# The first layer's expert outputs of three quads by way of DRAM rows instead of one-hot products

## The chip, the cores and the metric

One core of a Trainium2 chip runs the whole program. The metric is the device time of one execution in microseconds. The kernel before takes 940.01 us, the median of three runs (939.11 to 942.62).

## What is computed

Two trunk layers over 256 latent tokens (x) and 256 context tokens, 1024 channels, float32. Each layer ends in a mixture of experts; in the first layer all 512 tokens go through it. A token goes to one of four groups and to two of the group's four experts:

```python
eid = g * EXPERTS_PER_GROUP + ie                       # two experts of a token
gates = jnp.sum(jax.nn.one_hot(eid, N_EXPERTS) * wts[..., None], axis=1)
y = jnp.zeros_like(h)
for e in range(N_EXPERTS):
    a = jax.nn.silu(h @ w_gate[e]) * (h @ w_up[e])
    y = y + gates[:, e:e + 1] * (a @ w_down[e])
...
x = x + g2 * out[:B * N].reshape(B, N, D)
xc = xc + cg2 * out[B * N:].reshape(B, L, D)
```

An expert has 512 inner channels, so each of its three matrices is 2 MB and a layer's experts are 96 MB.

## The kernel before, in words

The change lies in `experts(l, ...)` with l = 0, the first layer. The 16 experts are taken in four **quads** q = 0 to 3 of four. A pair (token, expert) has a *slot*: an expert has 96, of which the first 64 of the four experts make slot tiles 0 and 1 of 128 rows, and the last 32 of each make tile 2. Tile 2 runs only where an expert of the quad has more than 64 pairs (`beyond(q)`, a branch; with these inputs in quads 1 and 2). Pairs beyond 96 are done after quad 1 by `overflow` (line 951), behind a branch on the count.

Per quad there are four chunks of 2 MB of gate weights (wg), four of up (wu) and four of down (wd). `weights` and `load` (line 108) fetch a chunk by a DMA on SP into a ring of five buffers and a sixth; a DMA into a buffer waits until PE has released what was in it six chunks ago. So SP runs at most six chunks ahead of PE.

`tiles` (line 1137) issues the products: gate into `ga`, then up into `ua`, then, after silu, product and transposes (line 172), down into `da`, one bank of 512 columns for each slot tile and half `hf` of the 1024 output channels. For a quad's inputs, `slots` (line 1066) builds a one-hot matrix `SS` of slot by token, `fetch` (lines 1079 to 1090) gathers the slots' rows of `h2d` in DRAM with indirect DMAs on POOL, and `turn` transposes them to channel-major `XT`.

The outputs go back to tokens with products. `halves` (lines 1253, 1254) splits a bank of `da` into a high part `oh` (ACT) and a low part `ol` (DVE), so that the product is exact. `combine` (line 1271) multiplies both parts by `SS`, 512 tokens at a time, which sums a token's two slots. `add` adds that into the channel-major x, times g2, with DVE (line 1291) or with ACT and POOL (lines 1288, 1289).

The order: a quad's first half is combined while its second half's down products run or right after them (line 1271 in the `if hf:` branch). Quad 1's second half is combined at once; those of quads 0 and 2 are left in `pending` and are emitted amid the next quad's gate products. Quad 3 goes by columns, and its combining is last. A scheduler places each instruction in an engine's queue; an engine runs its queue in order.

All weight DMAs are SP's; ACT issues a few of its own (rows of h2 to DRAM before the experts). Hardware-queue DMAs of SP and ACT share eight semaphores in turn, and a DMA waits for the one that had its semaphore before.

Of the kernel before, what the change touches and what calls it, by code (L numbers as in the profile page):

```python
# [36 lines left out]
EXTRA = 1  # slots for weights that the last layer's experts have besides the ring's and the early ones  # L37
CAP = {0: 96, 1: 64}

# columns of the packed small parameters  # L40
PAR_BMOD, PAR_NG, PAR_WR, PAR_BR, PAR_PSC = 0, 96, 128, 448, 488
PAR_W = 492
# columns of the constants that stay
CO_ID, CO_ONE, CO_TOK, CO_SLOT, CO_BEFORE, CO_BASE, CO_QUAD, CO_FIRST = 0, 128, 256, 768, 788, 804, 836, 840
CO_W = 844
# columns of the constants of the mixers
MC_ROT, MC_MASK = 0, 512
MC_W = 768
# columns of what pooling and the transform take, of both kinds
MB_POOL, MB_DFT, MB_CB, MB_PW, MB_FW = 0, 1088, 1600, 1856, 2112  # L50
BAND = 136  # tokens that a tile of 128 tokens reaches through the widest window
# columns of the per-layer parameters of the mixers
# [4 lines left out]
def build(tc, ctx, a, cap=CAP):  # L57
# [7 lines left out]
    shd = dram.tile([1, 2 * D], F32, name="shd")  # the first layer's second shift  # L65
    h2d = dram.tile([T, D], F32, name="h2d")  # rows of h2
    gd = dram.tile([T, 4], F32, name="gd")  # the slots and the gates
# [13 lines left out]
    class pinned:  # L81
        """an engine whose instructions stay in program order"""
# [37 lines left out]
    def load_split_parts(src, pinned=False, pool=None):  # L120
        """a generator of the two parts, after each chunk"""
# [25 lines left out]
    # the two streams, channel-major; the context's lives until the last layer has its keys and values  # L147
# [10 lines left out]
    count = cst.tile([P, 256], BF16, name="count")  # upper | ones, exact  # L158
# [15 lines left out]
    def keep_warm(n, bank=tmp):  # L174
        """products that nothing reads: TensorE's clock stays up over a wait"""
# [5 lines left out]
    def mod_stretch(l, st, pool, pinned=(), given=()):  # L181
        """a generator: yields after each piece of TensorE's work; given: pools for the first chunks, which are taken by
        themselves"""
# [25 lines left out]
        in_rows = l == 0 and st == 1  # the shift of the second norm goes to rows in DRAM  # L209
# [35 lines left out]
    class Squares:  # L245
        """sums of squares over the channels, taken as the chunks of x become final"""
# [27 lines left out]
        def rstd(self):  # L274
            """1 / rms of the tokens on their partitions"""
# [6 lines left out]
    def spread(out, x, pool, tag, bufs):  # L282
        """x [P, m] -> out [P, m * P]: the values along the free axis, on every partition"""
# [7 lines left out]
    # the first norm: h = x * rstd * s1 + sh in two parts  # L291
# [32 lines left out]
    def mixers(l, keep, pool, rb, w01, mods, box):  # L324
        """yields the chunks of x that are final"""
# [14 lines left out]
        def hs(k, t0, t1):  # L340
            """the two parts of tokens t0 .. t1"""
# [8 lines left out]
        # q | k | v, token-major  # L350
# [36 lines left out]
        # q and k: norm, rotary, to channel-major  # L387
        # q^T k of their parts: (hi lo) with (hi hi) and with (lo lo)
# [8 lines left out]
        def heads(tt):  # L397
# [13 lines left out]
            # the heads with their gains and, of the latents, turned  # L411
# [19 lines left out]
            # the parts: of k hi hi of each head, lo lo of each, of q lo hi | hi lo  # L431
# [29 lines left out]
        # pool | fourier, token-major  # L461
# [5 lines left out]
        # the rotary factors take the gains of q and k  # L467
# [8 lines left out]
        # after which products a tile's heads are turned  # L476
# [10 lines left out]
        # of the two tiles of a stream the transform takes the sum, for the even frequencies, and the difference, for the odd  # L487
# [9 lines left out]
        # attention: heads c and 4 + c, of the two kv heads, at a time  # L497
# [39 lines left out]
        def turned(tt, c, pr):  # L537
            """the probabilities with the keys on the partitions"""
# [14 lines left out]
        def attend():  # L553
# [3 lines left out]
            def start(i):  # L557
                """scores up to the i-th pair"""
# [84 lines left out]
        # output projection and gated residual: first the rows of pool and fourier, then attention's  # L643
# [25 lines left out]
    class Router:  # L669
        """logits = rstd * (x^T (s1 * w)) + sh^T w + b, taken as the chunks of x become final"""  # L670
# [682 lines left out]
    for l in range(L):  # L1353
# [8 lines left out]
        with phase(f"mix{l}", "right") as pool:  # L1362
# [49 lines left out]
            if l == 0:  # L1412
                drain(ro.plans)
# [164 lines left out]
```

## Time and profile before

| | |
|---|---|
| runs, median (range) | 940.01 us (939.11 to 942.62) |
| the profiled execution, its span from first to last instruction | 940.8 us |
| mean granted TensorE clock | 0.975 |
| busy: PE, DVE, ACT, POOL | 870.2, 410.6, 265.8, 64.3 us |
| DMA | 287.14 MB, mean 305 GB/s |
| quads 0, 1, 2, 3 of the first layer | 268.0 to 332.3, to 422.1, to 506.5, to 564.6 us |

The profile is one execution, whose span is the time that the sums below start from. PE is the matrix engine, PEld its weight load, DVE, ACT and POOL the vector, scalar and general engines, SP the one that issues the weight DMAs. A clock of 1.00 is TensorE's full speed. "idle before <-X" is idle time of an engine just ahead of an instruction and what ended it.

### The profile page before, as it was taken

To read this page: it belongs to the slowest core of one execution; us is meant where nothing else is said; L and a number is where in the kernel's file an instruction comes from. 1 tells how busy PE (TensorE), PEld (TensorE's weight loads), DVE (VectorE), ACT (ScalarE), POOL (GpSimd) and SP (SyncE) were. 2 spreads that over 40 slices of the span, in tenths; PEclk is the share of its full clock that TensorE was granted. 3 is DMA by queue.
4 is the path that set the end of the run, shared out by engine and by line. 5 is a ranking of instruction groups with operands and counts; after the bars stand their busy time and mean duration, and the time that the engine had idled before them with its cause. 6 is when DMAs were issued, how large, how long until landed. Compare 5 with 4: busy or idle time off the path is not lost. (4 is left out here: it accounts for less than half of the span.)

```text
span 940.8 us, 13190 instructions
## 1 busy us (share of the span) xinstructions
PE 870.2 (92%) x5078; PEld 480.7 (51%) x5078; DVE 410.6 (44%) x1028; ACT 265.8 (28%) x579; POOL 64.3 (7%) x74
## 2 busy tenths in 40 slices
PE   2899999999589999989999998989999999979998
PEld 2388666676253333442344446846874444424436
DVE  2285677723965240431122138877655231312212
ACT  4143667514421100110011035566432010101101
POOL 1000000001410030012001020000000000000000
PEclk9999999999599999999999997999999999989999
DMA  9636572653969999757966972894978999999981
GB/s 356 270 128 251 212 286 109 257 225 111 380 238 427 428 371 425 309 222 297 416 248 261 397 283 110 342 420 160 344 308 324 428 418 430 426 391 426 428 301 46
DMA packets 33393, 287.14 MB, mean 305 GB/s; under 512 B 3484, under 2 KB 13340, under 8 KB 16544
## 3 DMA queue, kind: packets, MB, share of 16 engines
q1 hardware_dynamic: 28736, 276.94, 73.5%
q0 software_dynamic: 1696, 5.79, 1.6%
q10 hardware_dynamic: 2880, 3.35, 1.0%
q8 instruction: 49, 0.80, 0.3%
q14 instruction: 32, 0.26, 0.1%
HBM read 282.90 MB, written 3.16 MB: 304 GB/s over the span
## 5 line engine op out<-in xcount | busy, mean ns | idle before, releaser
L1137 PE MATMUL acc<-w,XT 128*64 128x512 f32 (+1 forms) x768 | 173.0, 609 | 14.5 <-DVEq L951 11.0
L1137 PEld LDWEIGHTS acc<-w,XT 128*64 128x64 f32 (+1 forms) x768 | 53.0, 135 | 114.9 <-issue 102.5
L1137 PE MATMUL aux<-w,XT 128*64 128x512 f32 (+1 forms) x512 | 109.3, 593 | 0.6 <-PEq L1147 0.6
L1137 PEld LDWEIGHTS aux<-w,XT 128*64 128x64 f32 (+1 forms) x512 | 34.0, 130 | 65.6 <-issue 64.7
L1137 PE MATMUL acc<-w,x 128*64 128x512 f32 (+2 forms) x272 | 55.3, 575 | 2.9 <-PEq L1147 2.3
L193 PE MATMUL aux<-w,c 128*32 128x512 f32 x368 | 50.7, 671 | 2.4 <-DMA w<-w_mod 2.4
L1228 DVE SCALAR_TENSOR_TENSOR sg<-aux,gt,sg 128x512 f32<-128x512 f32 x12 | 9.0, 750 | 86.2 <-PE aux L1137 85.5
L115 DVE TENSOR_TENSOR wl<-w,wh 128x768 fp32r<-128x768 f32 (+2 forms) x48 | 43.7, 954 | 3.5 <-ACT wh L115 3.1
L1254 DVE TENSOR_TENSOR ol<-acc,oh 128x512 fp32r<-128x512 f32 (+1 forms) x25 | 15.7, 627 | 57.2 <-ACT oh L1253 57.0
L1253 ACT CAST oh<-acc 128x512 fp32r<-128x512 f32 (+1 forms) x25 | 13.4, 535 | 94.0 <-PE acc L1137 93.9
L115 ACT CAST wh<-w 128x768 fp32r<-128x768 f32 (+2 forms) x48 | 37.5, 831 | 7.7 <-DMA w<-w_out 4.1
L137 PE MATMUL acc<-wh,hh 128*128 128x512 f32 x96 | 38.6, 402 | 0.7 <-ACT hh L301 0.7
L139 PE MATMUL acc<-wh,hl 128*128 128x512 f32 x96 | 38.0, 396 | 0.0
L1193 ACT ACTIVATE sg<-acc 128x512 f32<-128x512 f32 x16 | 9.4, 597 | 100.9 <-PE acc L1137 100.9
L138 PE MATMUL acc<-wl,hh 128*128 128x512 f32 x96 | 37.8, 394 | 0.0
L526 ACT ACTIVATE pr<-acc,soft 128x512 f32<-128x512 f32 (+1 forms) x48 | 29.4, 619 | 11.7 <-DVE soft L523 11.7
L1137 PEld LDWEIGHTS acc<-w,x 128*64 128x64 f32 (+1 forms) x272 | 15.6, 130 | 32.5 <-issue 31.6
L1234 DVE SCALAR_TENSOR_TENSOR sg<-aux,gt,sg 128x512 f32<-128x512 f32 x2 | 1.5, 751 | 64.9 <-PE aux L1137 64.9
L1137 PE MATMUL aux<-w,aT 128*64 128x512 f32 (+2 forms) x192 | 29.1, 453 | 0.0
L1137 PE MATMUL acc<-w,aT 128*64 128x512 f32 (+1 forms) x160 | 28.8, 511 | 0.2 <-DVE aT L1225 0.2
L575 PE MATMUL aux<-pT,vt 128*64 128x128 f32 x320 | 27.3, 281 | 0.4 <-ACT pT L550 0.2
L1103 ACT COPY XT<-tmp 128x512 f32<-128x512 f32 x6 | 3.5, 585 | 81.5 <-PE tmp L172 81.5
(329 smaller groups left out, 1592.2 us busy)
## 6 DMA issues: line engine op xcount, KB each, us to landing
w<-wg SPq DMA_DIRECT2D x32, 2048.0 KB, 13.2
w<-wu SPq DMA_DIRECT2D x32, 2048.0 KB, 11.6
w<-wd SPq DMA_DIRECT2D x29, 2048.0 KB, 11.1
w<-w_mod SPq DMA_DIRECT2D x23, 2048.0 KB, 12.4
w<-w_out SPq DMA_DIRECT2D x4, 2048.0 KB, 8.4
w<-w_qkv SPq DMA_DIRECT2D x4, 1536.0 KB, 9.9
w<-wd SPq DMA_DIRECT2D x6, 1024.0 KB, 13.5
w<-w_pf SPq DMA_DIRECT2D x2, 2048.0 KB, 8.0
```

The costliest lines, as they stand in the source:

```text
L115: return S.copy(hi, x), eng.tensor_tensor(lo, x, hi.bitcast(F32), op=ALU.subtract)
L137: PE.matmul(out, lhs[0], rhs[0], start=start, stop=False, skip_group_check=True)
L138: PE.matmul(out, lhs[0], rhs[1], start=False, stop=False, skip_group_check=True)
L139: PE.matmul(out, lhs[1], rhs[0], start=False, stop=stop, skip_group_check=True)
L193: mm = PE.matmul(m[32 * j:32 * j + 32, :], sc2[:, k, :], w[:, kk, j * 512:(j + 1) * 512], start=(ch == chs[0] and kk == 0), stop=(ch == ch ...
L526: S.activation(pr[e], sp[e], AF.Exp, bias=nm[:, e:e + 1], scale=SCALE, accum_out=sums[:, e:e + 1])
L575: PE.matmul(o[e * 64:(e + 1) * 64, c * P:(c + 1) * P], vt[:, k0 + m, e * 64:(e + 1) * 64], pTs[e * nk + m], start=(m == 0), stop=(m == nk ...
L1137: PE.matmul(o, lh, r, start=(k == 0), stop=(k == last_k), skip_group_check=True)
L1193: S.activation(t, ga[st], AF.Silu)
L1228: V.scalar_tensor_tensor(sg[st], ua[st], gt[:, st:st + 1], sg[st], op0=ALU.mult, op1=ALU.mult)
L1253: S.copy(oh, da[st][:, c0:c1])
L1254: V.tensor_tensor(ol, da[st][:, c0:c1], oh.bitcast(F32), op=ALU.subtract)
```

## The change

A new DRAM tensor `yd` has 3 x 384 rows of 1024 channels and a row of zeros. For the first layer, quads 0 to 2 no longer split, combine and add: `store` copies each bank of `da` to SBUF (`ys`; tiles 0 and 2 with ACT, tile 1 with DVE) and writes it as 128 rows of 512 channels to `yd` with DMAs on ACT's queue, three of 256 KB for each half. `places` computes in the router, from the slots, the two rows of each token (the zero row where a pair is in quad 3 or beyond 96); nine small DVE instructions. In quad 3, `collect` does for each of four tiles of 128 tokens: two indirect DMAs on POOL, each fetching 128 rows of 4 KB from `yd`; one DVE addition of the two; eight PE transposes; eight DVE instructions of 128x128 that add the result times g2 into x. Quad 3 itself combines as before. The constants get 32 columns. The second layer and everything else compute as before.

```diff
+        def places(self, rk):
...
+            V.tensor_tensor(b, self.base, c16[1], op=ALU.add)
+            V.tensor_scalar(t, r, 64.0, None, op0=ALU.is_ge)
+            V.tensor_tensor(t, t, c16[0][:, None, :].to_broadcast([P, nt, 16]), op=ALU.mult)
+            V.tensor_tensor(t, t, r, op=ALU.add)
+            V.scalar_tensor_tensor(t, self.ov, 1e6, t, op0=ALU.mult, op1=ALU.add)
+            V.tensor_tensor(t, t, b[:, None, :].to_broadcast([P, nt, 16]), op=ALU.add)
+            V.tensor_tensor(m.rearrange("p (i t) c -> p i (t c)", i=2), self.M.rearrange("p (i t) c -> p i (t c)", i=2),
+                            t.rearrange("p t c -> p (t c)")[:, None, :].to_broadcast([P, 2, nt * 16]), op=ALU.mult)
+            V.tensor_reduce(f, m, axis=AX.X, op=ALU.add)
+            V.tensor_scalar(self.rows, f, float(YD), None, op0=ALU.min)
...
+        def collect(tts):
+            for tt in tts:
+                g = [pool.tile([P, D], F32, tag="xg", name="yr", bufs=3) for _ in range(2)]
+                for i in range(2):
+                    G.indirect_dma_start(out=g[i], out_offset=None, in_=yd[:, :],
+                                         in_offset=bass.IndirectOffsetOnAxis(ap=places[:, i * nt + tt:i * nt + tt + 1], axis=0))
+                V.tensor_tensor(g[0], g[0], g[1], op=ALU.add)
+                for i in range(2):
+                    t = tmp()
+                    for c in range(4):
+                        transpose(t[:, c * P:(c + 1) * P], g[0][:, (i * 4 + c) * P:(i * 4 + c + 1) * P])
+                    for c in range(4):
+                        k = i * 4 + c
+                        x = X[tt // 2][:, k, tt % 2 * P:tt % 2 * P + P]
+                        V.scalar_tensor_tensor(x, t[:, c * P:(c + 1) * P], modT[l][:, 40 + k, tt // 2:tt // 2 + 1], x,
+                                               op0=ALU.mult, op1=ALU.add)
...
                 drain(tiles([(ch * 2 + kk, XT[:, ch * 2 + kk, :], w[:, kk]) for kk in range(2)], KD - 1, ua,
                             ch % 2 == 0))
+                if l == 0 and q == 3 and ch < 2:
+                    collect(range(2 * ch, 2 * ch + 2))
...
+            def store(da, hf):
+                ys = pool.tile([P, nst, 512], F32, tag=("oh", "ol")[hf], name="ys", bufs=2)
+                def put(st, y):
+                    r0 = q * 384 + st * P
+                    nc.scalar.dma_start(yd[r0:r0 + P, hf * 512:(hf + 1) * 512], y)
+                for st in range(2):
+                    (V.tensor_copy if st else S.copy)(ys[:, st, :], da[st])
+                    put(st, ys[:, st, :])
+                with beyond(q) as there:
+                    S.copy(ys[:, 2, :], da[2])
+                    put(2, ys[:, 2, :])
+                with there.Else():
+                    put(2, ys[:, 0, :])
...
-            if q < 3:
+            if l == 0 and q < 3:
+                for hf in range(2):
+                    for c in range(2):
+                        down(da[hf], 2 * c, weights(wd(l, place[q], 2 * hf + c)))
+                    store(da[hf], hf)
+            elif q < 3:
```

What the scheduler makes of it is seen in three queues (the line numbers of the changed kernel are its own: 1162 there is 1137 before, 110 is 108). First PE, from the last down product of quad 2 (`x_2451` or `x_2462` holds the activations) into the gate products of quad 3 (`XT`, x8 is one chunk for two slot tiles; the rows of 32x512 are tile 2, which quad 3 skips). Before, the tail of quad 2's combining:

```order
L1271 MATMUL aux<-SS,oh 128x512
L1137 MATMUL acc<-w,XT 64x512 x8
L1271 MATMUL aux<-SS,ol 128x512
L1271 MATMUL aux<-SS,oh 128x512
L1271 MATMUL aux<-SS,ol 128x512
L867 TENSOR_LOAD plan
L1147 COMPARE_AND_BRANCH
L1137 MATMUL acc<-w,XT 32x512 x16
L1147 UNCONDITIONAL_BRANCH x2
L1137 MATMUL acc<-w,XT 64x512 x16
```

After the change, from that last down product:

```order
L1162 MATMUL aux<-w,x_2462 64x512
L1162 MATMUL acc<-w,XT 64x512 x8
L870 TENSOR_LOAD plan
L1172 COMPARE_AND_BRANCH
L1162 MATMUL acc<-w,XT 32x512 x16
L1172 UNCONDITIONAL_BRANCH x2
L1162 MATMUL acc<-w,XT 64x512 x8
L174 MATMUL tmp<-co,yr 128x128 x8
L1162 MATMUL acc<-w,XT 64x512 x8
L174 MATMUL tmp<-co,yr 128x128 x12
```

The combining is gone. The transposes of the fetched rows (`yr`, x8 is one tile of 128 tokens) stand between the gate chunks: those of tile 0 behind chunk 1, of tile 1 and half of tile 2 behind chunk 2, the rest behind chunk 3 and ahead of the up products.

Second POOL in quad 3: the eight fetches, with the semaphores that each waits for (DMAHW those of SP's and ACT's DMAs, DMASW those of POOL's).

```order
L1201 DMA yr<-yd,rows 128x1024 [waits DMAHW3_49,DMAHW2_49,DMAHW4_49,DMAHW1_49,DMAHW5_49,DMAHW0_49,DMAHW6_49,DMASW5_49,DMAHW7_49,DMASW3_49,PE_49]
L1201 DMA yr<-yd,rows 128x1024 [waits DMASW6_49,DMASW4_49,PE_49]
L1201 DMA yr<-yd,rows 128x1024 [waits DMASW7_49,DMASW5_49,PE_49]
L870 TENSOR_LOAD plan
L1172 COMPARE_AND_BRANCH
L1172 UNCONDITIONAL_BRANCH x2
L1201 DMA yr<-yd,rows 128x1024 [waits DMASW6_49,DMASW4_49,DVE_49]
L1201 DMA yr<-yd,rows 128x1024 [waits DMASW7_49,PE_49]
L1201 DMA yr<-yd,rows 128x1024 [waits DMASW6_49,DMASW0_49,DVE_49]
L1201 DMA yr<-yd,rows 128x1024 [waits DMASW1_49,DMASW0_49,DVE_49]
L1201 DMA yr<-yd,rows 128x1024 [waits DMASW2_49,PE_49]
```

The first waits for the stores. There are three buffers, so the fourth waits for DVE's first addition, the fifth for PE's transposes of tile 0, the sixth and the seventh for the second and the third addition, the eighth for the transposes of tile 1.

Third SP, the second to fourth gate chunk of quad 3. Before:

```order
L108 DMA w<-wg 128x4096 [waits DMAHW4_49,PE_49]
L1276 COMPARE_AND_BRANCH
L1276 UNCONDITIONAL_BRANCH x2
L108 ISA
L108 DMA w<-wg 128x4096 [waits DMAHW5_49,PE_49]
```

After:

```order
L110 DMA w<-wg 128x4096 [waits DMAHW4_49,PE_49]
L110 ISA
L110 DMA w<-wg 128x4096 [waits DMAHW5_49,DMAHW1_49,PE_49]
L870 TENSOR_LOAD plan
L1172 COMPARE_AND_BRANCH
L1172 UNCONDITIONAL_BRANCH x2
L110 ISA
L110 DMA w<-wg 128x4096 [waits DMAHW6_49,DMAHW2_49,PE_49]
```

SP and ACT draw on the same eight semaphores; after the change the first of these chunks, and others behind it, have a semaphore that a store had before, and wait for that store to land.

## Rows read from the trace of the kernel before

**Rows 1.** The page: PE's busy time and share of the whole span.

```profile
PE 870.2 (92%) x5078; PEld 480.7 (51%) x5078; DVE 410.6 (44%) x1028; ACT 265.8 (28%) x579; POOL 64.3 (7%) x74
```

**Rows 2.** Quads 0 to 3: length; busy PE, PEld, DVE, ACT, POOL; clock, DMA, GB/s.

```profile
268.00:332.30 64.30, 60.81 (x281) 25.15 (x281) 33.75 (x89) 9.50 (x16) 4.68 (x5) 1.00 0.92 378
332.30:422.10 89.80, 83.81 (x478) 32.66 (x477) 25.19 (x54) 10.07 (x19) 12.01 (x14) 0.99 0.83 333
422.10:506.50 84.40, 82.86 (x465) 31.29 (x465) 19.67 (x43) 8.18 (x15) 8.31 (x10) 0.97 0.78 309
506.50:564.60 58.10, 54.65 (x268) 25.08 (x267) 11.59 (x23) 11.07 (x25) 6.43 (x8) 1.00 0.84 322
```

**Rows 3.** The same view, cut where the DMA share changes.

```profile
290.00:385.00 95.00, 90.97 (x476) 32.87 (x472) 27.40 (x52) 8.18 (x15) 9.57 (x11) 1.00 0.98 413
385.00:435.00 50.00, 45.24 (x242) 19.39 (x242) 16.71 (x40) 6.36 (x12) 9.65 (x11) 0.93 0.60 214
435.00:475.00 40.00, 38.87 (x232) 12.67 (x229) 4.90 (x7) 2.29 (x4) 0.00 (x0) 1.00 0.98 410
475.00:515.00 40.00, 39.50 (x210) 17.84 (x211) 11.31 (x26) 6.36 (x12) 3.61 (x5) 1.00 0.63 234
```

**Rows 4.** The same view of line 1271 alone: PE and PEld busy, clock.

```profile
320.00:340.00 20.00, 9.28 (x32) 5.46 (x32) 1.00 0.96 409
394.00:420.00 26.00, 12.14 (x48) 8.70 (x48) 1.00 0.73 282
484.00:512.00 28.00, 12.37 (x48) 8.62 (x48) 1.00 0.66 256
```

**Rows 5.** Timeline of PE, quad 2's end to quad 3's up: start, us, instruction.

```profile
501.46 0.73 PE L1271 MATMUL tmp<-SS,oh 128*128 128x512 f32 x2
...
506.53 3.65 PE L1137 MATMUL acc<-w,XT 128*64 128x512 f32 x16
...
518.46 4.64 PE L1137 MATMUL acc<-w,XT 128*64 128x512 f32 x20
522.77 1.18 PE L1137 MATMUL aux<-w,XT 128*64 128x512 f32 x4
```

**Rows 6.** Timeline of DVE in the router.

```profile
250.63 0.21 DVE L89 TENSOR_TENSOR rw<-rw,acc 128x64 f32<-128x64 f32 x1
```

**Rows 7.** Timeline of PE after quad 1; last stands [idle before <-releaser].

```profile
422.16 2.83 PE L1137 MATMUL acc<-w,XT 128*64 128x512 f32 x6 [4.42 <-DVEq L951]
```

**Rows 8.** Groups of DVE instructions: busy us, mean ns of one, idle before.

```profile
L1105 DVE COPY XT<-tmp 128x512 f32<-128x512 f32 x12 | 8.1, 689 | 22.8 <-PE tmp L172 22.6
...
L262 DVE TENSOR_TENSOR part<-part,sq 128x512 f32<-128x512 f32 (+1 forms) x8 | 5.0, 626 | 10.3 <-POOL part L262 6.8 <-ACT sq L258 3.5
```

**Rows 9.** Timeline of POOL: a fetch behind another.

```profile
345.32 1.01 POOL L1090 DMA_INDIRECT xg<-h2d,ii  x1 [0.30 <-issue]
```

**Rows 10.** DMA issues of the span: count, KB each, median us to landing.

```profile
h2d<-xt ACTq DMA_DIRECT2D x2, 1024.0 KB, 16.4
...
gd<-small ACTq DMA_DIRECT2D x1, 8.0 KB, 3.4
```

**Rows 11.** DMA queues, 247 to 251 us, during a row store: packets, MB, share.

```profile
q1 hardware_dynamic: 108, 1.51, 88.4%
q10 hardware_dynamic: 105, 0.22, 13.8%
```

**Rows 12.** DMA issues, 342 to 366 us: a quad's fetches beside weights.

```profile
xg<-h2d,ii POOLq DMA_INDIRECT x3, 14.5
```

**Rows 13.** DMA issues, 424 to 436 us: a quad's fetches, weights mostly idle.

```profile
xg<-h2d,ii POOLq DMA_INDIRECT x3, 4.5
```

**Rows 14.** Timeline of PE: eight transposes.

```profile
470.23 1.06 PE L172 MATMUL tmp<-co,xg 128*128 128x128 f32 x8 [0.83 <-PE tmp L172]
```

**Rows 15.** Stretches after the stall of quad 1.

```profile
420.00:425.00 5.00, 2.84 (x8) 1.11 (x10) 2.81 (x8) 0.00 (x0) 1.16 (x2) 0.53 0.07 23
425.00:430.00 5.00, 5.00 (x30) 1.33 (x31) 1.92 (x6) 0.00 (x0) 3.78 (x5) 0.79 0.64 192
```

More of the change, by code (lines that the diff above doesn't have):

```diff
@@ L38 @@
 CAP = {0: 96, 1: 64}
+YD = 3 * 384
 PAR_BMOD, PAR_NG, PAR_WR, PAR_BR, PAR_PSC = 0, 96, 128, 448, 488
 PAR_W = 492
-CO_ID, CO_ONE, CO_TOK, CO_SLOT, CO_BEFORE, CO_BASE, CO_QUAD, CO_FIRST = 0, 128, 256, 768, 788, 804, 836, 840
-CO_W = 844
+CO_ID, CO_ONE, CO_TOK, CO_SLOT, CO_BEFORE, CO_BASE, CO_QUAD, CO_FIRST, CO_ROW = 0, 128, 256, 768, 788, 804, 836, 840, 844
+CO_W = 876
 MC_ROT, MC_MASK = 0, 512
@@ L67, in build @@
     gd = dram.tile([T, 4], F32, name="gd")
+    yd = dram.tile([YD + 1, D], F32, name="yd")
     def phase(name, side="left"):
@@ L763, in __init__ @@
             self.flag = small.tile([P, 1], I32, name="flag")
+            self.rows = small.tile([P, 2 * nt], I32, name="rows") if l == 0 else None
             self.plan = small.tile([P, 8], I32, name="plan")
@@ L885, in slots @@
                              m.rearrange("p (m c) -> p m c", c=16), axis=AX.X, op=ALU.add)
+        def places(self, rk):
+            nt = self.nt
+            c16 = [co[:, CO_ROW + i * 16:CO_ROW + (i + 1) * 16] for i in range(2)]
+            r = rk[:, 0:nt * 16].rearrange("p (t c) -> p t c", t=nt)
+            w = self.rt.work[:, 324:]
+            b = w[:, 0:16]
+            t = w[:, 16:80].rearrange("p (t c) -> p t c", t=nt)
+            m = w[:, 80:208].rearrange("p (m c) -> p m c", c=16)
+            f = w[:, 208:208 + 2 * nt]
+            V.tensor_tensor(b, self.base, c16[1], op=ALU.add)
[8 more added lines that the diff above has]
+            V.tensor_scalar(self.rows, f, float(YD), None, op0=ALU.min)
         def gates(self):
@@ L1045, in gather, with experts @@
                     V.tensor_scalar(XT[:, k, c0:c1], y[:, :W], sh[k], None, op0=ALU.add)
-    def experts(l, nt, h2, vec, gov, fv, place, more, XT, xpool, pool, where, last):
+    def experts(l, nt, h2, vec, gov, fv, place, more, places, XT, xpool, pool, where, last):
         n = nt * P
@@ L1167, in experts @@
             yg = itertools.cycle([x8[:, 1536:1792], x8[:, 1792:2048]])
+            z = pool.tile([P, D], F32, tag="xg", name="z", bufs=3)
+            G.memset(z[0:1, :], 0.0)
+            G.dma_start(yd[YD:YD + 1, :], z[0:1, :])
+        def collect(tts):
[14 more added lines that the diff above has]
+                                               op0=ALU.mult, op1=ALU.add)
         pending = []
@@ L1188, in experts @@
                     rows(range(2, 4))
-                    SS, _ = slots(0, False)
+                    SS = None if l == 0 else slots(0, False)[0]
             sg = []
@@ L1413, in build @@
                 drain(ro.plans)
+                ro.places(rk)
             next(filler, None)
@@ L1451, in build @@
                 where = itertools.cycle([ring] * 5 + ([spare] * EXTRA + early if l else slot0))
-                nxt = experts(l, nt, None if l == 0 else h2, vec, gov, fv, place, more, XT, hp, pool, where, l == L - 1)
+                nxt = experts(l, nt, None if l == 0 else h2, vec, gov, fv, place, more, ro.rows, XT, hp, pool, where, l == L - 1)
         rp_stack.close()
@@ L1473, in constants @@
     co[:, CO_FIRST:CO_FIRST + 4] = [-100, 1, 2, 3]
+    j = np.arange(16) % 4
+    co[:, CO_ROW:CO_ROW + 16] = 192 - 32 * j
+    co[:, CO_ROW + 16:CO_ROW + 32] = -32 * j - 1
     mc = np.zeros((P, MC_W), f)
```

## The prediction

> **What bounds the kernel now.** I began with the page. TensorE (PE) is busy 92% of the span [rows 1], so the first question of any removal is whether it takes work from PE. The stretches of the first layer's four quads (a quad is four experts) come next [rows 2]: PE is busy 60.8 of 64.3 us, 83.8 of 89.8, 82.9 of 84.4 and 54.7 of 58.1. In the first three quads PE sets the pace, and work taken from it there should come off the time, as long as the weights keep up. So the DMA share is what to read second [rows 3]: 0.98 from 290 to 385 us, 0.60 to 435, 0.98 to 475, 0.63 to 515. The weight stream is close behind PE, but it has slack: 2% of 95 us, 40% of 50, 2% of 40 and, up to the end of quad 2's down products at 501.5 us, 37% of 26.5, together 32.5 us.
>
> Two places matter. One is the combining by one-hot products, line 1271, which has its own rows [rows 4]: PE is busy with it for 9.28 us in quad 0, 12.14 in quad 1 and 12.37 in quad 2. The other is the passage from quad 2 to quad 3 [rows 5]. Quad 2's down products end at 501.46. PE then combines quad 2's second half and runs the gate products of quad 3 between and after that; at 518.46 begins a row of 20 of which the first 16 are gate (3.4 us), so the up products start at 521.9. **From the end of quad 2's down to quad 3's up it takes 20.4 us**, and PE hardly waits. Everything behind that point, quad 3's up and down, its own combining and layer 1, keeps its order. So the time changes by what happens to the moment at which quad 3's up can start.
>
> **The change part by part.** *Removed before 501.46.* Quads 0 and 1 whole and the first half of quad 2: 9.28 + 12.14 + 6.2 (half of 12.37) = **27.6 us** of PE. The vector work that goes with it (the split in two halves, the additions into x) hangs on these products and lies beside other PE work: nothing of its own.
>
> *Added in the router.* Nine small DVE instructions compute the row numbers. A similar one takes 0.21 us [rows 6]; 1.9 us if all delay the one-hots that PE waits for, 0 if DVE has gaps there. I take 1.9.
>
> *The weights.* PE wants them 27.6 us sooner, and five halves of three 256 KB stores, 3.9 MB, are added by then: 9.5 us at the 413 GB/s of the saturated stretch [rows 3]. 27.6 + 9.5 = 37 us are taken from 32.5 us of slack. Ring buffers that are less full at the end can lend the missing 4.6 us; some landings will still be late, and SP's next gate chunk also waits now for an earlier store's landing, since both queues share landing semaphores. Between 0 and 8 us late; I take 3.
>
> *A wait that stays.* After quad 1 PE stands 4.42 us until DVE reaches a branch [rows 7]. The combining ahead of it goes, but PE gets there sooner too. Kept; at best 4.4 us are gained.
>
> So quad 2's down products end at 501.46 - 27.6 + 1.9 + 3 = **478.8 us** (470 to 486).
>
> *The new chain behind it.* In place of the combining, quad 3's gate has transposes of fetched rows in its PE queue: chunks 0 and 1 can run, then PE stands until the first tokens are there; the last transposes stand directly ahead of up. The first fetch on POOL waits for all stores. Its steps, from the end of quad 2's down:
> 1. Two copies on one engine, at most 0.69 us each by DVE's [rows 8], and three issues: 1.4 us alone, 4.4 if an issue costs the 1.0 of POOL's [rows 9]. I take 2.3.
> 2. Three stores of 256 KB land. A store of 1024 KB in rows took 16.4 us beside weights; the smallest one, 8 KB, 3.4 [rows 10]. Three quarters of 16.4 are 12.3. In the busiest stretch the store's queue moved 0.22 MB in 4 us while the weights moved 1.51 [rows 11], which gives 14.3. Between 3.4 and 14.3; I take 12.3, because weights stream at that time: SP runs up to six chunks ahead of PE, and PE frees two more. Now at +14.6.
> 3. Two fetches of 512 KB for the first 128 tokens. The same kind from the rows of h2 took 14.5 us beside weights [rows 12] and 4.5 with weights mostly idle [rows 13]; a second one is issued 1.3 us after the one ahead of it [rows 9]. Between 5.8 and 14.5; again the loaded one. At +29.1.
> 4. DVE adds the two rows, 128x1024: twice the 0.626 us of 128x512 [rows 8], 1.25. At +30.4.
> 5. There are three buffers for eight fetches. The fourth waits for the first addition, the sixth for the second, the seventh for the third. That makes three more rounds of one fetch and one addition in series: 5.8 us each with idle weights, 15.8 beside them. Eight chunks of 2.1 MB at 413 GB/s last 41 us at most; then about one round of the three still falls beside weights, at 12 between the two prices, and two do not: 12 + 2 x 5.8 = 23.6 (17.4 to 47). At +54.0. Gate chunks 2 and 3 run inside these rounds.
> 6. Eight transposes, 1.06 us [rows 14], twice that at half clock: 2.1. Up starts at **+56.1** (31 to 80) instead of +20.4.
>
> That is 478.8 + 56.1 = 534.9, against 521.9: 13.0 us later. After the 4.4 us stall PE's granted clock was 0.53 of full speed for 420 to 425 and 0.79 for the next 5 us [rows 15], that is, part of them at 1.2 GHz; 0.47 of 2.84 busy us and 0.21 of 5 are 2.4 us. After this far longer stall the same is to be paid: +2.4 (0 to 4). Against it, in quad 3 PE is not busy for 58.1 - 54.65 = 3.45 us [rows 2]; with weights that had time to arrive I give back 1.5 (0 to 3.45).
>
> **The sum:** +13.0 + 2.4 - 1.5 = +13.9 us on the profiled execution's 940.8, which lies 0.8 above the median of the runs, 940.01. From that median: 953.9, **954 us**. 27.6 us come off, and the wait for the last quad's tokens is longer than what came off. A chain of 42 us would leave the time as it is (521.9 - 478.8, less the 0.9 of clock and weights).
>
> **The rivals.** *The transfers go at their idle price (faster).* The place is steps 2, 3 and 5; it decides if the weights have been fetched before the stores are issued, or if a store and a fetch are not slowed by them. For it: quad 2 has a DMA share of 0.78, and the fetches at 424 us took 4.5 us [rows 2, 13]. Then the chain is 2.3 + 3.4 + 5.8 + 1.25 + 17.4 + 1.1 = 31.2 us, up starts at 510.0, and with clock and weights the time is 940 - 11.9 + 0.9 = 929 us. Against it: PE is sooner at that point while the weights are not, so more of them lie ahead there than before. [...] Chance of this rival 0.21.
>
> *Gain and wait cancel.* With one price idle and the other loaded, for instance stores at 12.3, the first pair at 7.5 and all rounds at 5.8, the chain is 42 us: 940 us, within 0.5%. Chance 0.19.
>
> *The weights hold PE back as well.* The slack of 32.5 us cannot all be used, since a buffer is only refilled after PE has released it. Then the weights are 10 us late and not 3 by the end of quad 2, with the same chain behind: 954 + 7 = 961 us. For it speak the two stretches at 0.98 [rows 3]; against it that PE was busy 91.0 of 95 us in one of them. Chance 0.12.
>
> **How the numbers follow.** My forecast has 0.48, the late weights 0.12: slower by over 0.5% (4.7 us, about what a measurement of this kernel can tell from no change) 0.60. Within 0.5%: 0.19. Faster: 0.21. The range from 930 to 967 reaches from the rival at idle price to late weights with 6 us more for the rounds; outside it lie the faster half of the first rival and a chain whose rounds all run beside weights (+23 us). For the slower cases alone it is 945 to 967.
>
> **What would show it.** In the new profile the end of quad 2's down products should stand near 479 us, with no products of combining before it but for quad 3's own. Then PE runs two gate chunks, and two or three idle stretches on PE follow whose releaser is DVE's addition or POOL's fetches; they sum to some 35 us. The granted clock falls to 0.5 there. POOL issues three fetches and then single ones, about 6 to 12 us apart, and up begins near 535 us. The last stores should take over 10 us to land, the first pair of fetches over 10 us. I am wrong if the fetches land in 4 to 5 us each, if PE is idle for less than 20 us between down and up, or if PE waits for weights in quads 1 and 2 for more than 8 us.

## The result and the profile after

The changed kernel takes **965.0 us**, the median of four runs (962.9 to 966.76), beside 940.2 us for the kernel before on the same chip: a ratio of 1.0242, 95% interval 1.0221 to 1.0263. It is slower by 24.8 us. The profiled execution has a span of 961.1 us, 20.3 more than before; the step by step comparison below is made on that. The 4.5 us that are left lie between the profiled executions and the medians of the runs: the profiled execution after took 962.9 us, the least of its four, and the one before, by its span of 940.8, seems to be that of 942.62 us, the most.

PE's busy time fell as meant, by 25 us [rows 1]. The page, PE's line and the DMA queues of POOL (q0) and ACT (q10):

```profile
PE 845.4 (88%) x4982; PEld 462.9 (48%) x4982; DVE 399.4 (42%) x1024; ACT 255.2 (27%) x558; POOL 62.9 (7%) x69
...
q0 software_dynamic: 2880, 9.99, 3.1%
q10 hardware_dynamic: 5472, 8.07, 2.3%
```

The timeline of PE, from the stand after quad 1 to the start of quad 3's up, answers to [rows 5, 7]. At the end of a row stands the idle time ahead of it and what ended it:

```profile
404.58 7.84 PE L1162 MATMUL acc<-w,XT 128*64 128x512 f32 x32 [7.39 <-DVEq L976]
...
477.40 3.60 PE L1162 MATMUL acc<-w,XT 128*64 128x512 f32 x16
481.16 3.65 PE L1162 MATMUL acc<-w,XT 128*64 128x512 f32 x16 [0.16 <-PEq L1172]
513.35 1.97 PE L174 MATMUL tmp<-co,yr 128*128 128x128 f32 x8 [28.53 <-DVE yr L1203]
...
526.19 1.12 PE L174 MATMUL tmp<-co,yr 128*128 128x128 f32 x4 [4.15 <-DVE xl L1211]
...
539.35 2.15 PE L174 MATMUL tmp<-co,yr 128*128 128x128 f32 x8 [5.32 <-DVE yr L1203]
541.44 1.56 PE L1162 MATMUL acc<-w,XT 128*64 128x512 f32 x4
```

Quad 2's down products end at 477.4 us, 24.1 earlier than before, and two gate chunks follow at once. Then PE stands 28.5 us for the first tokens, and twice more for others. Quad 3's up begins at 541.4, 64.0 us after the end of quad 2's down; before, it was 20.4. From there to the end it is 419.7 us, 418.9 before. So the whole loss is made between these two points: 24.1 us won up to the first, 43.6 lost behind it. (4.0 of the 24.1 were won before quad 0 began, see below.)

The stretches of the same piece (length, busy PE, PEld, DVE, ACT, POOL, clock, DMA share, GB/s):

```profile
404.60:477.40 72.80, 71.32 (x420) 23.34 (x422) 7.57 (x11) 4.68 (x9) 0.00 (x0) 0.97 0.82 336
477.40:541.40 64.00, 25.42 (x98) 10.50 (x94) 13.21 (x39) 1.63 (x3) 7.50 (x8) 0.69 0.82 330
...
485.00:513.35 28.35, 0.00 (x1) 0.00 (x1) 1.23 (x1) 0.00 (x0) 2.82 (x3) 0.55 0.94 396
```

While PE stands, the DMA engines are 94% busy. The timeline of POOL shows the fetches, that of DVE the additions that release PE:

```profile
500.20 0.94 POOL L1201 DMA_INDIRECT yr<-yd,rows  x1 [98.39 <-DMA w<-wu]
...
513.56 0.94 POOL L1201 DMA_INDIRECT yr<-yd,rows  x1 [9.93 <-DVE yr L1203]
...
519.53 0.94 POOL L1201 DMA_INDIRECT yr<-yd,rows  x1 [3.00 <-DVE yr L1203]
525.37 0.94 POOL L1201 DMA_INDIRECT yr<-yd,rows  x1 [4.90 <-DVE yr L1203]
...
```

```profile
512.07 1.23 DVE L1203 TENSOR_TENSOR yr<-yr 128x1024 f32<-128x1024 f32 x1 [33.31 <-DMA yr<-yd,rows]
...
538.07 1.22 DVE L1203 TENSOR_TENSOR yr<-yr 128x1024 f32<-128x1024 f32 x1 [9.60 <-DMA yr<-yd,rows]
```

Three fetches go out together from 500.2, the others as additions free a buffer: the three serial rounds of the prediction. The first fetch's wait is put down to a weight chunk, the last event in that row. The stores' queue (q10) has its last packets between 498.5 and 499.0 us, just ahead of the fetch at 500.2, and in the fifth and sixth experiment, where the landing of the last store is on record, the first fetch follows it by 1.0 and 1.1 us. So it is the store that it waits for; the second experiment tests it.

The DMA queues (q1 weights, q10 stores) and the stores' median time to landing, first for quad 2's first half, 466 to 470 us, then for its second, 477 to 500 us:

```profile
q10 hardware_dynamic: 383, 0.72, 48.2%
...
yd<-ys ACTq DMA_DIRECT2D x3, 256.0 KB, 2.3
```

```profile
q1 hardware_dynamic: 615, 9.03, 91.9%
q10 hardware_dynamic: 432, 0.79, 9.0%
...
yd<-ys ACTq DMA_DIRECT2D x3, 256.0 KB, 15.2
```

Three stores of 256 KB land in 2.0 to 2.5 us with no weight packet in the row. Ten microseconds later, beside 9 MB of weights, the one landing of the three that the trace has, that of the second store, took 15.2 us; by the queue's last packets the third took about 20. Why the weights are all there at that moment is seen in SP's queue, and in what SP waited for from 440 to 480 us:

```profile
444.25 27.30 SPq L110 DMA_DIRECT2D w<-wg  x4
472.33 21.66 SPq L110 DMA_DIRECT2D w<-wu  x4
...
SPq L110 <- DMA yd<-ys: 24.2, 1, 24.2
```

Of the four gate chunks of quad 3 the first is issued at 444.25 and the other three between 469.4 and 471.2, behind the landing of the first of the first half's stores at 469.3. That is the wait on a shared semaphore: SP stands 24.2 us for a store. The next up chunk follows at 472.3, so four chunks of 2 MB leave within 3 us, just ahead of the second half's stores at 477.9.

### The profile page after: what moved, and what is told of

It reads as the page before. It is cut to its first block, busy times and chain, and to the rows that moved or that the text cites. A ratio compares the mean times of both kernels' runs of the same rounds, so it can differ in the third digit from the quotient of the medians.

```text
span 961.1 us, 12877 instructions
## 1 busy us (share of the span) xinstructions
PE 845.4 (88%) x4982; PEld 462.9 (48%) x4982; DVE 399.4 (42%) x1024; ACT 255.2 (27%) x558; POOL 62.9 (7%) x69
## 5 line engine op out<-in xcount | busy, mean ns | idle before, releaser
L1162 PE MATMUL acc<-w,XT 128*64 128x512 f32 (+1 forms) x768 | 177.5, 621 | 18.0 <-DVEq L976 13.8
L117 DVE TENSOR_TENSOR wl<-w,wh 128x768 fp32r<-128x768 f32 (+2 forms) x48 | 43.6, 954 | 2.6 <-ACT wh L117 2.2
L174 PE MATMUL tmp<-co,yr 128*128 128x128 f32 x32 | 7.2, 377 | 38.3 <-DVE yr L1203 33.9
L1301 ACT CAST oh<-acc 128x512 fp32r<-128x512 f32 (+1 forms) x14 | 6.9, 495 | 81.6 <-PE acc L1162 81.5
## 6 DMA issues: line engine op xcount, KB each, us to landing
w<-wg SPq DMA_DIRECT2D x32, 2048.0 KB, 13.9
```

The source lines that it names most:

```text
L1162: PE.matmul(o, lh, r, start=(k == 0), stop=(k == last_k), skip_group_check=True)
```

## The experiments

The theory after the result (W): the time is lost where quad 3's gate stands for the last stores and for fetches in series, not on PE's work and not in the weight stream of quads 0 to 2. The rival (D): PE, once freed of products, outruns the weights, beside which the DMA engines have to carry 9 MB more; the stand only shows it. A third (L): the shared semaphores make the transfers collide. Each run is compared with the kernel before on its own chip (941.6 to 942.2 us there); a difference to the change is that of two such differences.

**1. No fetching.**

```diff
-                if l == 0 and q == 3 and ch < 2:
-                    collect(range(2 * ch, 2 * ch + 2))
```

> The changed kernel without the fetching in quad 3 (no fetches, additions, transposes; the outputs of quads 0 to 2 are stored and never added, so that part of the result is left out). Theory W (the time is lost where quad 3's gate stands for stores and fetches in series): PE runs quad 3's gate and up without that stand, only weights can hold it there; up begins near 493 us in place of 541, quad 3 ends 20 to 25 us before the kernel before, and the time is about 918 us (912 to 926). Theory D (the earlier pace outruns the weight stream, and the bytes of the stores cost what the products cost): PE waits for weights in its place; the time is 935 us or more.

Measured: 920.3 us, ratio to before 0.9765 (0.9731 to 0.98). W gives the time to within 3 us. Its timeline of PE in quad 3, and the stretch from the end of quad 2's down to the end of up:

```profile
492.53 1.08 PE L1162 MATMUL acc<-w,XT 128*64 128x512 f32 x4 [1.94 <-DMA w<-wu]
...
507.56 1.08 PE L1162 MATMUL acc<-w,XT 128*64 128x512 f32 x4 [1.19 <-DMA w<-wu]
```

```profile
475.40:512.00 36.60, 29.52 (x134) 9.48 (x130) 2.55 (x10) 1.52 (x3) 0.00 (x0) 1.00 1.01 428
```

Without the fetching 46 of the change's us are gone; with the wait went also 32 transposes and the fetched bytes. And D is not nothing: PE now waits 1.2 to 1.9 us for each up chunk at a DMA share of 1.01. There is no free transfer time in this stretch for 4.2 MB of fetches, 10 us at that rate.

**2. Quad 2 stored where nothing reads it.**

```diff
-                    r0 = q * 384 + st * P
-                    nc.scalar.dma_start(yd[r0:r0 + P, hf * 512:(hf + 1) * 512], y)
+                    r0 = q % 2 * 384 + st * P
+                    nc.scalar.dma_start((yd2 if q == 2 else yd)[r0:r0 + P, hf * 512:(hf + 1) * 512], y)
```

> The changed kernel with quad 2's outputs stored to a DRAM tensor that nothing reads, so that the fetches wait for quads 0 and 1 alone; quad 2's outputs are left out of the result. All else, bytes and PE's work too, stays. Theory W: the first three fetches go as soon as their buffers are free in quad 2's down (near 460 us), so the stand of 28.5 us at tile 0 is gone; three rounds of one fetch and one addition beside weights (11 to 12 us each) are left, and up begins near 505 to 515 us instead of 541: 930 to 938 us. If the last stores' landing is not what the first fetch waits for (it could be a weight chunk on a shared semaphore), the stand stays and the time is 955 us or more.

Measured: 939.4 us, ratio 0.9973 (0.9956 to 0.9989), 27 us less than the change: a little above the expected 930 to 938, far from 955. The transposes of the first and the last two tiles on PE:

```profile
468.86 1.06 PE L175 MATMUL tmp<-co,yr 128*128 128x128 f32 x8 [0.41 <-ACT ys L1324]
...
488.79 1.97 PE L175 MATMUL tmp<-co,yr 128*128 128x128 f32 x8 [4.17 <-DVE yr L1204]
...
503.37 1.97 PE L175 MATMUL tmp<-co,yr 128*128 128x128 f32 x8 [8.54 <-DVE yr L1204]
```

The stand of 28.5 us is gone with the wait for quad 2's stores; the stands of the later rounds, up to 8.5 us, stay. Bytes and PE's work are the same. So it is the last stores that the first fetch waits for. Without that wait, and with all fetches earlier for it, the kernel is 27 us faster, which is about the whole loss.

**3. Eight buffers.** The rows of tiles 0 and 1 go to the three buffers of before and one of `SS`, those of tiles 2 and 3 to space of the split halves.

```diff
-                g = [pool.tile([P, D], F32, tag="xg", name="yr", bufs=3) for _ in range(2)]
+                g = [room("yr") for room in rooms[2 * tt:2 * tt + 2]]
```

> The changed kernel with eight buffers for the eight fetches instead of three (space that quad 3 does not use then); no fetch waits for an addition. Theory W: the fetches go out 1.25 us apart behind the last store and land together; the first addition stays near 512 to 514 us, the last comes near 520 instead of 538, and up begins near 524 us: 945 us (940 to 951). If the fetches take their time from the bytes that flow at once and not from the order in which they may start, the later ones land no sooner: 957 us or more.

Measured: 952.7 us, ratio 1.0119 (1.0078 to 1.016), some 14 us less than the change, between the two expectations. The fetches' landing, and PE's last transposes:

```profile
DMA to landing us min/median/max: 10.5/10.6/10.7
```

```profile
513.55 1.97 PE L174 MATMUL tmp<-co,yr 128*128 128x128 f32 x8 [28.56 <-DVE yr L1212]
...
530.10 1.09 PE L174 MATMUL tmp<-co,yr 128*128 128x128 f32 x8
531.12 1.08 PE L1162 MATMUL acc<-w,XT 128*64 128x512 f32 x4
```

All eight land within 20 us of the first issue, as W says, and up begins at 531.1 instead of 541.4. I had expected 524: behind the first addition PE still has two gate chunks and 32 transposes to do, 17.6 us from 513.55 to 531.12; up to 520 us the granted clock is 0.50 of full speed, that is 1.2 GHz. The serial rounds cost 10 us, and with them gone PE's own work is next.

**4. Quads 0 and 1 only, quad 2 by products.**

```diff
-YD = 3 * 384
+YD = 2 * 384
...
-            if l == 0 and q < 3:
+            if l == 0 and q < 2:
```

> Only quads 0 and 1 go by way of DRAM; quad 2 combines by products as in the kernel before. The result is whole. Theory W: the fetched rows were stored a quad earlier, so no fetch waits for a store; 21.4 us of products go, 32 transposes of 4.3 us come, and the fetches begin when their buffers are free near 465 us; what is left of the rounds may hold PE a little in quad 3's gate: 922 to 934 us, faster than both kernels. Theory D: weights hold PE back by what was saved: 938 us or more.

Measured: 944.9 us, ratio 1.0022 (0.9999 to 1.0044): no change against before, and W's expectation missed by over 10 us. The number lies on D's side. The last large stand on PE, POOL's sixth fetch, and all that PE waited for weights from 270 to 530 us:

```profile
508.37 1.12 PE L174 MATMUL tmp<-co,yr 128*128 128x128 f32 x4 [9.36 <-DVE xl L1211]
```

```profile
494.46 0.95 POOL L1201 DMA_INDIRECT yr<-yd,rows  x1 [5.39 <-PEq L1172]
...
PE acc L1162 <- DMA w<-wu: 0.4, 1, 0.4
```

No fetch waits for a store, but there are still three buffers; the sixth fetch goes out at 494.5 and lands 11.6 us later, and PE stands 9.4 us for it. So the number is D's and the mechanism is not: PE waits 0.4 us for weights. The sixth fetch goes out behind PE's transposes of the first tile, which free its buffer and stand in quad 3's gate. Not the store alone decides, but also the place at which PE asks for the rows.

**5. Stores on POOL.**

```diff
-                    nc.scalar.dma_start(yd[r0:r0 + P, hf * 512:(hf + 1) * 512], y)
+                    G.dma_start(yd[r0:r0 + P, hf * 512:(hf + 1) * 512], y)
```

> The changed kernel with the 18 stores issued by POOL instead of ACT, so that SP's weight DMAs no longer share semaphores with them. Theory L (the shared semaphores held SP back from 444 to 469 us, and the four to five chunks that then went out at once are what the last stores and the first fetches collide with): gate chunks of quad 3 go out one by one from about 445 us, the last stores land in under 8 us instead of 15 to 21, the first fetches in 5 to 8, and up begins near 510 to 520 us instead of 541: 930 to 940 us. Theory C (stores and fetches collide with the weights of quad 3 in any case): the last stores still land over 12 us after their issue, 950 us or more.

Measured: 950.6 us, ratio 1.0082 (1.0056 to 1.0108), 16 us less than the change. SP's queue, then the first fetch on POOL and the landing times from 477 to 500 us, then the last stand on PE:

```profile
444.69 23.13 SPq L110 DMA_DIRECT2D w<-wg  x4
472.77 12.85 SPq L110 DMA_DIRECT2D w<-wu  x4
```

```profile
495.26 0.99 POOL L1201 DMA_INDIRECT yr<-yd,rows  x1 [15.04 <-DMA yd<-ys]
...
yd<-ys POOLq DMA_DIRECT2D x3, 256.0 KB, 11.7
yr<-yd,rows POOLq DMA_INDIRECT x3, 7.2
```

```profile
532.19 1.97 PE L174 MATMUL tmp<-co,yr 128*128 128x128 f32 x8 [10.14 <-DVE yr L1203]
```

The gate chunks leave one by one, at 444.7, 450.0, 462.2 and 467.5, so L is right on the cause of the burst. The first fetches land in 7.2 us instead of 10.5 and the first is issued 5 us sooner. But the stores still take 9 to 15 us and the time is C's, 950 us or more; the last round now falls beside the down chunks (13.5 us to landing). Both hold in part: the burst makes a collision worse that is there without it.

**6. The merging behind quad 3's up.** Eight buffers as in 3, with the additions and transposes put into PE's and DVE's written order between the down products.

```diff
-                if l == 0 and q == 3 and ch < 2:
-                    collect(range(2 * ch, 2 * ch + 2))
+                if l == 0 and q == 3:
+                    fetch_rows(ch)
...
                             down(da[hf], 2 * c, weights(wd(l, place[q], 2 * hf + c)))
+                            if l == 0:
+                                collect(2 * c)
+                                collect(2 * c + 1)
```

> Eight buffers as in the third experiment, and the additions and transposes of the fetched rows put behind quad 3's up products, between the first down products, in PE's written order. Theory W: PE does gate and up while stores and fetches land; no stand of over 10 us is left between quad 2 and quad 3's down, and 32 transposes of 4.3 us remain against the kernel without fetching: 924 to 936 us, faster than before. If the transfers merely take the place of the weights, up is held back by late weight chunks instead: 940 us or more.

Measured: 939.7 us, ratio 0.9977 (0.9947 to 1.0007): 27 us less than the change, no difference to before, and above the 924 to 936 expected. The stretch of quad 3's gate and up, and the landing of the fetches:

```profile
481.00:520.00 39.00, 29.70 (x133) 9.57 (x129) 3.21 (x10) 1.38 (x3) 7.51 (x8) 1.00 1.01 424
```

```profile
DMA to landing us min/median/max: 11.1/19.8/21.4
```

The stand is gone from PE's gate. In its place stands what experiment 1 showed coming: a DMA share of 1.01 from 481 to 520 us, fetches that take up to 21 us, and two stands of 4.1 and 2.9 us in the down. In this arrangement, with the wait hidden and the stores on ACT, three quads by DRAM cost what the products cost.

**7, 8, 9. Two quads, the fetches moved.** In 7 the rows are fetched and merged in quad 2's up, into space of the split halves. In 8 the stores are POOL's too, and DVE's products of quad 0's activations stay ahead of the one-hots for quad 2. In 9 (stores on ACT) tiles 0 and 1 are merged in quad 2's up, tiles 2 and 3 in quad 3's gate and up. Of the lines below the first three stand in all of them, the next two in 9, the last two in 8 and 9.

```diff
+            if l == 0 and q == 2:
+                fetch_rows(0)
+                fetch_rows(1)
...
+                if l == 0 and q == 2 and ch > 1:
+                    collect(ch - 2)
...
-                V.scalar_tensor_tensor(sg[st], ua[st], gt[:, st:st + 1], sg[st], op0=ALU.mult, op1=ALU.mult)
+                (pinned(V) if l == 0 and q == 0 else V).scalar_tensor_tensor(sg[st], ua[st], gt[:, st:st + 1], sg[st], op0=ALU.mult, op1=ALU.mult)
```

> Quads 0 and 1 by way of DRAM, quad 2 by products, and the rows fetched and added during quad 2's up products, in PE's written order, into buffers that are free then (those of the split halves). The result is whole. Theory W: no wait for a fetch is left on PE (under 5 us); 21.4 us of products go, 4.3 us of transposes come, and the 3 us longer stand after quad 1 and some 4 us lost in quad 0 stay: 924 to 932 us. If the bytes that are added cost as much as the products did, 938 us or more.

> As the seventh, with the stores on POOL (nothing of them on SP's semaphores), and with DVE's products of quad 0's activations kept ahead of the one-hots for quad 2 (in the changed kernel the scheduler puts those ahead, and PE stands 3.75 us for the activations at 303 us, then runs at half clock for a while). The result is whole. Expected: the stand at 303 us is gone, 4 us, and weights come no later than before: 918 to 927 us. If the order on DVE was not the cause, PE still stands there.

> Quads 0 and 1 by way of DRAM, quad 2 by products, stores on ACT. Tokens of tiles 0 and 1 are fetched in quad 2's gate and added behind the last two up chunks of quad 2; those of tiles 2 and 3 are fetched in quad 2's down, when three more buffers are free, and added behind gate chunk 2 and up chunk 0 of quad 3; DVE's order in quad 0 as in the eighth. The result is whole. If what kept the fourth and the seventh from gaining was only when PE asked for the rows, no stand of over 3 us is left but the one after quad 1: 924 to 933 us, faster than before. If it is the bytes (8.7 MB less the part of quad 2 that the weight stream has no room for), PE waits for weight chunks or rows elsewhere: 936 us or more.

Measured: 951.3 us, ratio 1.0102 (1.0058 to 1.0145); 944.0, 1.002 (0.9994 to 1.0046); 942.9, 1.0002 (0.9978 to 1.0025). All three miss, and 7 and 9 lie where their expectations put the price of the bytes. But from 270 to 530 us PE waits for weights not at all in 7 and 8 and 0.7 us in 9; what it stands for is rows. In 7 the stands have moved with the merging (PE, then the landing of the fetches):

```profile
440.47 1.97 PE L174 MATMUL tmp<-co,yr 128*128 128x128 f32 x8 [8.42 <-DVE yr L1209]
...
463.85 2.15 PE L174 MATMUL tmp<-co,yr 128*128 128x128 f32 x8 [8.70 <-DVE xl L1218]
```

```profile
DMA to landing us min/median/max: 7.7/11.2/21.8
```

Quad 1's last stores, issued from 396.8 us, land in 17.4 us in the median: four chunks have left together just ahead of them, from 390.5 to 393.4, as in the change. In 8 the stand of quad 0 is gone, as expected, and those in quad 2's up are there still, 5.5 and 8.1 us. In 9 two stands of over 2 us are left besides the one after quad 1: 5.2 us in quad 2's up and 4.9 at 497.6, which is met again in 10.

**10, 11. The split merging with stores on POOL, then DVE's order as well.** 10 is 9 with POOL's stores. In it PE stands for a split of quad 2's second half that is queued on DVE behind an addition that waits for rows; 11 orders these.

```profile
491.62 1.22 PE L1354 MATMUL tmp<-SS,ol 128*128 128x512 f32 x2 [5.04 <-DVE ol L1320]
```

```diff
-            V.tensor_tensor(g[0], g[0], g[1], op=ALU.add)
+            tc.keep_in_program_order(V.tensor_tensor(g[0], g[0], g[1], op=ALU.add))
...
-                    V.tensor_tensor(ol, da[st][:, c0:c1], oh.bitcast(F32), op=ALU.subtract)
+                    (pinned(V) if l == 0 and q == 2 else V).tensor_tensor(ol, da[st][:, c0:c1], oh.bitcast(F32),
+                                                                          op=ALU.subtract)
```

> As the ninth, with the stores issued by POOL, so that they share no semaphores with SP's weight DMAs. If the bursts of weight chunks behind the shared semaphores still cost something there, 2 to 5 us less than the ninth; if not, within 1 us of it.

> As the tenth, with DVE's additions of fetched rows kept behind the splits of quad 2's halves in DVE's order. In the tenth PE stands 5.04 us at 491 us for a split that is queued on DVE behind an addition that waits for a fetch, and runs at half clock after it. Expected: that stand is gone, 5 to 8 us less than the tenth: 927 to 931 us. If the fetch's bytes hold the weights back there instead, within 2 us of the tenth.

Measured: 935.4 us, ratio 0.9907 (0.9878 to 0.9937), and **925.9 us, ratio 0.9837 (0.9813 to 0.9861)**. The stores' queue is worth 7.5 us, more than the 2 to 5 expected, and DVE's order 9, more than the 5 to 8 expected. In 11 no stand of over 1 us is left from quad 2's up to quad 3's; the longest in quad 2's combining, and the stretch of 480 to 505 us:

```profile
483.00 0.73 PE L1355 MATMUL tmp<-SS,ol 128*128 128x512 f32 x2 [0.89 <-DVE ol L91]
```

```profile
480.00:505.00 25.00, 23.81 (x109) 11.10 (x107) 8.02 (x24) 3.68 (x7) 3.45 (x4) 1.00 0.80 314
```

This version is faster than both kernels, by 16 us than before.

**12. DVE's order in quad 0 alone**, in the changed kernel: the last line of the diff of 7 to 9, and with it the one-hots for quad 2, which are held in the written order too (8 to 11 have this line as well).

```diff
-                V.tensor_scalar(t, bc[0], s_, None, op0=ALU.is_equal)
+                (pinned(V) if l == 0 and q == 2 else V).tensor_scalar(t, bc[0], s_, None, op0=ALU.is_equal)
```

> The changed kernel with only DVE's order in quad 0 changed: the products of its activations stay ahead of the one-hots for quad 2. If PE's stand of 3.75 us at 303 us and the half clock after it come from that order and are not taken up by a later wait, 3 to 5 us less than the changed kernel: 960 to 962 us. If a later wait (the weights, the branch after quad 1) takes it up, 964 us or more.

Measured: 962.5 us, ratio 1.0209 (1.019 to 1.0229), 4 us less than the change by the two differences; the intervals of the two ratios overlap slightly. PE at the same point, in the changed kernel and here:

```profile
303.60 1.97 PE L174 MATMUL tmp<-co,sg 128*128 128x128 f32 x8 [3.75 <-DVE sg L1276]
```

```profile
301.09 1.04 PE L1162 MATMUL acc<-w,x 128*64 128x512 f32 x2 [0.83 <-issue]
```

The stand goes, and nothing later takes it up: the stand for the first tokens is 28.6 us, as in the changed kernel, and ends 2.9 us sooner.

## Why the prediction was right, and where its sizes were off

The forecast was 954 us and the measured time is 965.0, within the range and 2 us from its upper end. The way of the loss was right and its size too small: 13.9 us forecast, 20.3 on the profiled executions, 24.8 on the medians.

**The bound and the removal.** Right in kind. 27.6 us of products went, and quad 2's down ends at 477.4 us where 478.8 were forecast. That the two are so near is in part luck, for the parts of it were not as I had them. Quad 2 is shorter by 6.5 us: 72.8 from 404.58 to 477.40, 79.3 before [rows 5, 7]. Quads 0 and 1 lost 21.4 us of products but only 13.6 of length, 140.6 us from the first gate product at 263.96 to 404.58 against 154.2 [rows 2, 7]. Three of the 7.8 us that came back are the longer stand after quad 1, 7.39 against 4.42: PE got there 20.6 us sooner and the branch came only 17.6 sooner. The next largest is new, 3.75 us at 303.6 and a granted clock of 0.64 from there to 308.2: as no `SS` is built for quad 0, its buffer is free and the scheduler builds that of quad 2 there, ahead of quad 0's activations on DVE; experiment 12 takes this order away and the stand with it. Of the stand after quad 1 I had kept the 4.4 us and not its growth; the other I had not named. Against that, quad 0 began 4.0 us sooner, although the router had more to do; the charge of 1.9 us for it cannot be seen. 1.8 of the 4.0 are there ahead of the router (one and the same product of it begins at 234.32 before and at 232.50 after), and in the traces of the twelve experiments, none of which changes the router, the first gate product begins anywhere from 261.6 to 265.7. So part of these 4.0 us may be the scatter of single executions; without them quad 2's down would have ended at 481.4. The weights were late by 1.5 us at one chunk, not 3.

**The chain.** Right in kind at each of its steps. Steps 3 to 6, measured and forecast: the first pair took 11.9 us to the addition (14.5 forecast), the addition 1.23, the three rounds 26.1 from 513.3 to 539.4 (23.6), the last transposes 2.15 (2.1). **The step that was mis-sized is step 2**, the landing of the last stores: the first fetch left 22.8 us after quad 2's down, not 14.6. At 12.3 us, and 14.3 at most, I had the last stores too cheap: the last of them took about 20. What is on the way at this place is four chunks that the shared semaphore had held back and let go at once, and I had the shared semaphores as a delay of weights, not as the burst that the stores meet. In experiment 5, with the stores on POOL and without the burst, the first fetch leaves 17.4 us after quad 2's down (477.84 to 495.26): 5.4 of the missing 8.2 us go with it, 2.8 remain. The chain came out 7.9 longer (64.0 against 56.1), as the other steps cancel. With 1.4 us gained ahead of it the sum is 20.3 instead of 13.9 on the profiled span.

**The last two terms.** +2.4 for the clock and -1.5 for weights that had time to arrive: their sum of 0.9 meets the 0.8 that was lost behind the start of up, but by luck. The granted clock is 0.89 for the first 4.6 us of up and 1.00 from there, which is 0.5 us; before that the slow clock, 0.74 from 513.3 to 541.4, falls into the rounds, where PE waits in any case. And nothing was given back: from the start of up to the last combining product quad 3 takes 43.3 us, 42.8 before.

**The rivals.** *Idle prices* was wrong for this kernel and is where the prices belong: stores of 2.3 us and fetches of 4.3 us are in its trace, at the places without weights. *Late weights* forecast 961 us, nearer to the 965.0 than my own number, but its mechanism did not happen: PE waits 1.5 us for weights in quads 0 to 2. Experiments 1 and 6 show that it is next in line: with the wait hidden, quad 3's gate and up are at a DMA share of 1.01. The 27.6 us of products were not to be had in full: experiment 1, which fetches nothing at all, is 21.3 us faster than before, and experiment 6, which hides the fetches, ends where the products ended.

**A fetch alone and in a stream.** By the fit in the Trainium skill, page "DMA: Bandwidth & Descriptors", section "Anatomy of one DMA — SWDGE (gpsimd) path", a DMA issued by POOL takes about 2.0 us plus its bytes at 436 GB/s, which makes a fetch of 512 KB an estimated 3.2 us. The changed kernel's single fetches take 4.3 us with few weights beside them, the first three 10.5, and those of experiment 6 up to 21.4. In these traces the fit is a floor, and beside the weight stream the price is up to seven times as much. The fit is for POOL's path, so it does not price the stores, which ACT issues.

What stays open: the price of the fetched bytes alone, without their wait, was not measured by itself, and neither was the change with the stores' bytes taken away. Experiment 6 was not run with the stores on POOL and DVE's order in quad 0, which gave 16 and 4 us in the changed kernel, so that three quads by DRAM cannot beat the products is not shown. The 4.0 us by which quad 0 began sooner are not explained beyond the above.

## What to carry to other kernels

In this kernel work taken off a busy engine was worth its time only up to the next point at which that engine waits; the first question for a detour through DRAM is who asks for the data, when, and what else is on the DMA queues then. Fetch what was written a stage ago and not what was written just now, put the consumer where the landing lies behind it, and look through every queue that the wait enters: here POOL's three buffers (14 us), DVE's order (4 and 9) and the stores on ACT, which shares semaphores with SP (16 and 7.5), each cost time of their own. A transfer's price is the one beside the traffic at its own place, not that of the same transfer elsewhere.

## What the runs showed of the hardware that was not expected

While both had work, the queue of the weights and that of the stores shared the engines by packets and not by bytes. From 494 to 497 us of the changed kernel:

```profile
q1 hardware_dynamic: 74, 1.21, 94.2%
q10 hardware_dynamic: 73, 0.15, 12.8%
```

One packet of a store, as the profile counts them, against one of a weight chunk, and an eighth of the bytes; [rows 11] had the same, 105 against 108. It agrees with what the Trainium skill states, page "DMA: Bandwidth & Descriptors", section "Queues, rings and completion order": an engine goes round the queues by packets. A store in rows of 2 KB beside 16 KB packets of weights got 50 GB/s (0.15 MB in 3 us) while the engines moved 454.

In experiment 3 eight fetches issued one behind the other took no longer each than three in the changed kernel, 10.6 us against 10.5. POOL issued them 1.24 us apart, and so they landed, which is 512 KB at some 420 GB/s; the DMA share was 0.97 from 508 to 512 us. The pace of POOL's issues and the rate of the engines are about the same here, and which of the two set it is not shown.
